# When the stores of a streaming attention kernel are let go: in pairs, each pair behind the K load eight groups later, instead of only the last nine, behind the last K load

## The chip, the cores and the metric

The kernel runs on one core of one Trainium2 chip. The metric is device time in microseconds (us). A program on one core is timed several times. The profiled execution has a "span" of its own, from its first to its last instruction; it is 1.8 us shorter than the device time in most kernels here, and 2.0 to 2.1 us in four of them (see e11). In the profile PE is TensorE (matrix products; PEld are its weight loads), DVE is VectorE, ACT is ScalarE, POOL is GpSimd and SP is SyncE, which only issues transfers here.

## The reference

```python
def reference(Q, K, V):                       # each (8, 12, 512, 64), float32
    Q_feat = np.maximum(0, Q)
    K_feat = np.maximum(0, K)
    KV = np.einsum('bhkd,bhkv->bhdv', K_feat, V)
    K_sum = np.sum(K_feat, axis=2)
    numerator = np.einsum('bhqd,bhdv->bhqv', Q_feat, KV)
    denominator = np.einsum('bhqd,bhd->bhq', Q_feat, K_sum)
    return (numerator / (denominator[:, :, :, None] + 1e-10)).astype(np.float32)
```

The work is light: 37.75 MB are read, 12.58 MB are written, and each byte is used once.

## The kernel before

The 96 heads are worked in 24 groups of four. A group has three loads (K, V, Q, each 512 KB of float32 in HBM, cast to bf16 on the way in) and one store (512 KB). The loads are issued by GpSimd, except for K and V of the first two groups; there are 14 buffers of each kind, so they run far ahead of the compute. The last step of a group is its "norm": DVE divides by the denominator and writes the output tile, which is then stored. The stores are issued by SP, in order.

```python
    HELD = 7
    # ...
    outp = pool("outp", HELD + 4)
    # ...
    for g in range(F32):                       # groups 0 and 1 come in as float32
        k_sb[g] = outp.tile([P, R, D], fp32, name="k_first", tag="o_sb")
        nc.sync.dma_start(out=k_sb[g]..., in_=Kr[g])
        # ... V likewise, issued by ACT
    # ...
    for g in range(2, NG - 2):
        load_kv(g)
        load_q(g)
    load_kv(NG - 2); load_kv(NG - 1); load_q(NG - 2); load_q(NG - 1)
    # ...
    def store(g, o_sb):
        if g == NG - 2 - HELD:                                     # g == 15
            nc.sync.dma_start(out=scratch, in_=k_sb[NG - 1][0:1, 0, :])
        parts = 2 if g >= NG - 3 else 1
        n = R // parts
        for j in range(parts):
            rs = slice(n * j, n * (j + 1))
            nc.sync.dma_start(out=Or[g].rearrange(...)[:, rs], in_=o_sb[:, rs])
    # ...
    for g in range(NG):
        mm_kv(g); evac_kv(g)
        # ... prep(g + 1): relu of K and copy of V, on DVE
        if g > 0:
            mm_out(g - 1)
            store(g - 1, norm(g - 1))
        transp(g); evac_qt(g)
    mm_out(NG - 1)
    store(NG - 1, norm(NG - 1))
```

The line with `scratch` is a gate. It copies 128 bytes of a K tile to a tile nobody reads. The copy has to wait until that tile is loaded, and since SP issues in order, all stores behind it wait too. Before, stores 0 to 14 go as soon as they are computed; stores 15 to 23 wait for K23, the last K load.

## Time and profile before

| | before |
|---|---|
| device time, median of the first runs | 130.9 us |
| busy share of the span: PE, DVE, ACT | 56%, 62%, 39% |
| share of the chain of waits that is DMA | 79% |
| K8 / K22 / K23 landed at | 42.7 / 109.7 / 112.9 us |
| first store issued at | 16.0 us |
| last norm ends at | 122.7 us |
| last store lands at | 128.4 us |

The first fence is from the profile page of the kernel before. It has the strips of 40 slices (3.2 us each) with the DMA engines' busy tenths and GB/s, the chain of waits by engine, and two DMA queues. q0 are the loads from GpSimd, q1 all that SP issues.

```profile
DMA  3999999999999999999999999999999999989991
GB/s 115 385 291 210 208 186 277 283 224 274 235 260 275 232 274 260 236 286 244 252 286 231 264 274 232 276 259 237 285 212 208 208 212 207 207 262 395 404 390 75
...
q0 software_dynamic: 9792, 17.83, 74.2%
q1 hardware_dynamic: 4208, 13.63, 27.9%
...
DMA 79%; DVE 5%; PE 3%; POOL 3%; issue 2%; ACT 2%; POOLq 0%; ACTq 0%
```

DMA is busy for eight tenths or more of every slice but the first and the last. The GB/s of the strip count a cast load at its bf16 size, so 210 for loads alone is 420 GB/s read from HBM; stores count once. Read so, loads alone and stores alone move nearly the same HBM bytes per us.

The second fence is from the table by stretches of time, kernel before. After the stretch come its length, the busy us and number of instructions of PE, PEld, DVE, ACT and POOL, and the granted clock. The last two columns, the ones used here, are the DMA share and GB/s. The share adds up the times of all packets of the sixteen engines, and these overlap a little, so it can pass 1.

```profile
18.00:20.00 2.00, 1.20 (x52) 0.71 (x44) 1.56 (x4) 1.56 (x5) 0.53 (x1) 1.00 1.10 155
43.30:93.90 50.60, 31.88 (x719) 23.62 (x720) 31.90 (x90) 20.67 (x50) 16.39 (x30) 0.53 1.10 259
98.40:112.90 14.50, 11.03 (x272) 8.18 (x270) 12.33 (x36) 7.83 (x19) 3.75 (x8) 0.61 1.12 210
113.00:114.00 1.00, 0.44 (x20) 0.23 (x16) 1.00 (x3) 0.39 (x2) 0.00 (x0) 1.00 0.73 135
114.00:115.00 1.00, 0.16 (x3) 0.17 (x4) 0.93 (x5) 0.00 (x0) 0.00 (x0) 1.00 0.69 195
...
118.00:122.00 4.00, 1.71 (x39) 1.18 (x36) 2.76 (x10) 1.02 (x1) 0.00 (x0) 0.50 1.01 402
122.00:124.00 2.00, 0.00 (x0) 0.00 (x0) 0.67 (x1) 0.00 (x0) 0.00 (x0) 0.50 1.02 389
...
126.00:127.00 1.00, 0.00 (x0) 0.00 (x0) 0.00 (x0) 0.00 (x0) 0.00 (x0) 0.50 0.64 244
127.00:128.00 1.00, 0.00 (x0) 0.00 (x0) 0.00 (x0) 0.00 (x0) 0.00 (x0) 0.50 0.07 27
```

Two dips stand out. At 18 to 20 us only loads run, at 155 instead of 210. The DMA share stays at 1.10 there, so the engines are not empty. At 113 to 115 us the share does fall, to 0.73 and 0.69: loads are running out, and the held stores have not begun. At the very end, 127 to 128, 27 GB/s is about the rate of a single engine, by an estimate from the 400 that sixteen make.

The third fence is SP's timeline of the kernel before (start, duration, what). It shows the gate.

```profile
0.74 0.86 SPq L87 DMA_DIRECT2D k_first<-in_K_dram  x2
15.95 71.68 SPq L184 DMA_DIRECT2D out_dram<-o_sb  x15
112.91 0.62 SPq L179 DMA_DIRECT2D scratch<-k_sb  x1
113.62 11.43 SPq L184 DMA_DIRECT2D out_dram<-o_sb  x12
```

### The profile page before, as it was taken

What the parts mean: (1) busy time and instruction counts of PE and PEld (TensorE: products, weight loads), DVE (VectorE), ACT (ScalarE), POOL (GpSimd) and SP (SyncE); (2) the same over time, 40 slices, a digit from 0 to 9 for tenths busy, and PEclk for the clock granted to TensorE, in tenths of its full rate; (3) what the DMA queues carried; (4) which work ended last, traced back from release to release, by engine and by line L of the source; (5) the groups of instructions that cost most, each with busy time, mean ns of one, the idle gap of its engine ahead of it and who ended that gap; (6) DMA issues with size and microseconds to landing.
All of it is one profiled execution on the core that took longest, in us unless ns stands there. A gap on an engine that the chain in (4) does not pass through costs nothing.

```text
span 129.3 us, 4118 instructions
## 1 busy us (share of the span) xinstructions
PE 73.0 (56%) x1728; PEld 54.3 (42%) x1728; DVE 80.5 (62%) x230; ACT 51.0 (39%) x121; POOL 39.2 (30%) x74
## 2 busy tenths in 40 slices
PE   0037982628565573585585665854856888556300
PEld 0036752416443452463364454533643656434200
DVE  1358883736757658458467576584586898897600
ACT  3034763333354335334533543353335366536000
POOL 6905343133433324315133333141333431000000
PEclk9999999755568559555555555555555555995555
DMA  3999999999999999999999999999999999989991
GB/s 115 385 291 210 208 186 277 283 224 274 235 260 275 232 274 260 236 286 244 252 286 231 264 274 232 276 259 237 285 212 208 208 212 207 207 262 395 404 390 75
DMA packets 14305, 32.76 MB, mean 253 GB/s; under 512 B 1616, under 2 KB 1616, under 8 KB 14288
## 3 DMA queue, kind: packets, MB, share of 16 engines
q0 software_dynamic: 9792, 17.83, 74.2%
q1 hardware_dynamic: 4208, 13.63, 27.9%
q10 hardware_dynamic: 288, 1.05, 2.1%
q8 instruction: 13, 0.21, 0.6%
q14 instruction: 4, 0.03, 0.1%
HBM read 37.75 MB, written 12.58 MB: 389 GB/s over the span
## 4 chain that ended last, share of the span: by engine, by line
DMA 79%; DVE 5%; PE 3%; POOL 3%; issue 2%; ACT 2%; POOLq 0%; ACTq 0%
DMA v_sb<-in_V_dram 41%; DMA q_sb<-in_Q_dram 27%; DMA k_sb<-in_K_dram 11%; DVE o_sb L168 2%; ACT qt L143 2%; PE ps_out L154 1%; POOL q_sb L82 1%; PE ps_qt L139 1%; DVE vo L116 1%; DVE rec L167 1%; PE ps_kv L124 1%; POOL k_sb L76 1%; POOL v_sb L78 1%; DVE den L165 0%; POOL ident masks.py:199 0%
## 5 line engine op out<-in xcount | busy, mean ns | idle before, releaser
L124 PE MATMUL ps_kv<-vo,kf 64*128 64x65 bf16 x768 | 23.3, 228 | 33.6 <-DVE vo L116 33.4
L133 ACT CAST kvd<-ps_kv 64x130 bf16<-64x130 f32 x96 | 25.4, 264 | 32.7 <-PE ps_kv L124 30.7
L143 ACT ACTIVATE qt<-ps_qt 128x1024 bf16<-128x1024 bf16 x24 | 24.6, 1024 | 34.4 <-PE ps_qt L139 34.4
L124 PEld LDWEIGHTS <-kf 64*128 64x128 bf16 x768 | 19.7, 119 | 39.2 <-DVE vo L116 31.5
L154 PE MATMUL ps_out<-kvd,qt 128*32 128x130 bf16 x768 | 27.9, 296 | 12.0 <-DVE o_sb L168 7.1
L168 DVE TENSOR_TENSOR o_sb<-ps_out,rec 128x512 f32<-128x512 f32 x48 | 33.2, 692 | 1.7
L114 DVE TENSOR_SCALAR kf<-k_sb,mask 128x1024 bf16<-128x1024 bf16 x44 | 19.4, 483 | 21.5 <-DMA k_sb<-in_K_dram 21.4
L154 PEld LDWEIGHTS <-qt 128*32 128x32 bf16 x768 | 17.1, 124 | 20.4 <-DVE o_sb L168 12.1
L82 POOL DMA_DIRECT2D q_sb<-in_Q_dram x24 | 15.2, 632 | 32.1 <-DMA k_sb<-in_K_dram 16.0
L139 PE MATMUL ps_qt<-ident,q_sb 128*128 128x128 bf16 x192 | 23.6, 299 | 2.2 <-DMA q_sb<-in_Q_dram 2.2
L139 PEld LDWEIGHTS <-q_sb 128*128 128x128 bf16 x192 | 17.5, 135 | 6.7 <-issue 3.8
L78 POOL DMA_DIRECT2D v_sb<-in_V_dram x22 | 11.7, 531 | 18.5 <-DMA q_sb<-in_Q_dram 11.2
L76 POOL DMA_DIRECT2D k_sb<-in_K_dram x22 | 11.9, 540 | 16.8 <-DMA v_sb<-in_V_dram 7.1
L116 DVE COPY vo<-v_sb 128x1024 bf16<-128x1024 bf16 x22 | 9.5, 430 | 9.4 <-DMA v_sb<-in_V_dram 9.4
L167 DVE RECIPROCAL rec<-den 128x8 f32<-128x8 f32 x48 | 9.8, 203 | 1.7
L165 DVE TENSOR_SCALAR den<-ps_out 128x8 f32<-128x8 f32 x48 | 7.6, 158 | 1.6 <-PE ps_out L154 1.6
L114 DVE TENSOR_SCALAR kf<-k_first,mask 128x1024 bf16<-128x1024 f32 x4 | 2.8, 750 | 5.3 <-DMA k_first<-in_K_dram 5.3
L133 ACT ACT_TABLE_LOAD x1 | 1.3, 1283 | 1.7 <-DVE kvd L107 1.7
L116 DVE CAST vo<-v_first 128x1024 bf16<-128x1024 f32 x2 | 1.4, 692 | 0.0
L105 DVE MEMSET mask<- 32x1 f32 x8 | 0.3, 59 | 0.9 <-PEq L216 0.8
L107 DVE MEMSET kvd<- 128x260 f32 x3 | 0.8, 275 | 0.0
masks.py:199 POOL TENSOR_SCALAR_AFFINE_SELECT ident<-ident 128x128 bf16<-128x128 bf16 x1 | 0.3, 287 | 0.1
(6 smaller groups left out, 0.8 us busy)
## 6 DMA issues: line engine op xcount, KB each, us to landing
out_dram<-o_sb SPq DMA_DIRECT2D x21, 512.0 KB, 6.7
q_sb<-in_Q_dram POOLq DMA_DIRECT2D x24, 256.0 KB, 12.4
k_sb<-in_K_dram POOLq DMA_DIRECT2D x22, 256.0 KB, 13.7
v_sb<-in_V_dram POOLq DMA_DIRECT2D x22, 256.0 KB, 13.4
out_dram<-o_sb SPq DMA_DIRECT2D x6, 256.0 KB, 4.2
v_first<-in_V_dram ACTq DMA_DIRECT2D x2, 512.0 KB, 6.6
k_first<-in_K_dram SPq DMA_DIRECT2D x2, 512.0 KB, 6.3
scratch<-k_sb SPq DMA_DIRECT2D x1, 0.1 KB, 3.3
```

What stands on the lines that cost most here:

```text
L76: nc.gpsimd.dma_start(out=k_sb[g].rearrange("p r d -> p (r d)"), in_=Kr[g])
L78: nc.gpsimd.dma_start(out=v_sb[g].rearrange("p r d -> p (r d)"), in_=Vr[g])
L82: nc.gpsimd.dma_start(out=q_sb[g].rearrange("p u f -> p (u f)"), in_=Qr[g])
L114: nc.vector.tensor_scalar(kf[g][:, :, s, :], k_sb[g], scalar1=0.0, scalar2=mask[:, s:s + 1], op0=Alu.max, op1=Alu.mult)
L116: nc.vector.tensor_copy(vo[g % NB][:, :, 0:D], v_sb[g])
L124: nc.tensor.matmul(ps_kv[g][:, t, 0:D1], kf[g][ts_, r, :, :].rearrange("p s d -> p (s d)"), vo[g % NB][ts_, r, :], start=(r == 0), stop=(r ...
L133: nc.scalar.copy(kvd[g % NB][64 * c:64 * c + 64, :, s, c, :], ps_kv[g][64 * s:64 * s + 64, :, 0:D1])
L139: nc.tensor.transpose(ps_qt[g][:, u, :], q_sb[g][:, u, :], ident)
L143: nc.scalar.activation(qt[g].rearrange("p u q -> p (u q)"), ps_qt[g].rearrange("p u q -> p (u q)"), Act.Relu)
L154: nc.tensor.matmul(po[hs, v // 2, (v % 2) * 2 * D1:(v % 2) * 2 * D1 + 2 * D1], qt[g][:, u, hs], kvd[g % NB][:, h // 2, h % 2, :, :], start ...
L167: nc.vector.reciprocal(rec, den)
L168: nc.vector.tensor_tensor(o_sb[:, 8 * j:8 * j + 8].rearrange("p (b r) d -> p b r d", b=2), pv[:, :, :, 0:D], rec.unsqueeze(3).to_broadcast ...
```

## The change

Its intent is to hold every store back a little, and to let none wait for the very end. Even-numbered stores 0 to 14 each get a gate on the K load eight groups later; the odd one behind it follows freely. So stores go in pairs from K8 on, and everything from store 14 on is free once K22 has landed. The output pool grows by one buffer, and the store of group 20 is split in two like those after it.

```diff
-    HELD = 7
+    DELAY = 8
...
-    outp = pool("outp", HELD + 4)
+    outp = pool("outp", DELAY + 4)
...
     def store(g, o_sb):
-        if g == NG - 2 - HELD:
-            nc.sync.dma_start(out=scratch, in_=k_sb[NG - 1][0:1, 0, :])
-        parts = 2 if g >= NG - 3 else 1
+        if g + DELAY < NG and g % 2 == 0:
+            nc.sync.dma_start(out=scratch, in_=k_sb[g + DELAY][0:1, 0, :])
+        parts = 2 if g >= NG - 4 else 1
```

## The prediction

> **What bounds the kernel now.** The DMA engines. The 40-slice strip shows DMA at 9 tenths from the second slice to the last but one; PE is busy 56%, DVE 62%, ACT 39%; the chain of waits is 79% DMA. A 512 KB transfer costs about the same in every phase, by the spacing of the K loads in the timeline: loads alone (K19 to K23) take 3.75 us a group of three, 1.25 us each; loads with one store a group (K8 to K18) 5.12 us, so a store costs 1.37 us; the nine held stores at the end run at 390 to 407 GB/s, 1.31 us each. HBM traffic is about 414 GB/s with and without stores. The Trainium skill's page "DMA: Bandwidth & Descriptors" (section "Queues, rings and completion order") says each engine round-robins between queues by packet; the trace agrees: with both busy, loads get about 195 GB/s of reads and stores 203.
>
> **What the change does.** It removes no byte. It adds 7 dummy transfers of 128 B (eight for one), each behind a K load. It splits the store of group 20: half stores run at 390 GB/s against 401, about 0.04 us. It moves work:
> - Before, stores 0 to 14 go as they are computed, from 16.0 us; 15 to 23 wait for K23, which lands at 112.9.
> - After, loads run alone up to K8: K2 at 12.1 + 6 x 3.75 = about 34.6 us, against 42.7 before. Then stores go in pairs, two for six loads, 10.2 us a pair; K22 lands at about 109 (109.7 before), and stores 14 to 23 follow freely.
>
> **How much is critical.** The order of transfers changes, not their sum, so little. To be won:
> 1. At the hand-over (113 to 115.5) the DMA rate falls to 194 to 304 GB/s: loads run dry before the held stores start, as K23's landing is seen late and a store's data comes about 1 us after its issue. Worth about 0.7 us. After, stores are released 3 us earlier, with V22 to Q23 in flight, so this dip should go.
> 2. A dip at 18 to 20 us (about 300 GB/s, 0.5 us lost), which may vanish or recur elsewhere.
>
> Against this: packets end at 126.5 on all but one engine, at 128.1 on a straggler. If that engine never starved in the dips, filling them gains nothing. I count half of the 0.7 us. At the end, Q23 shares with stores and lands at about 117.5 to 118 instead of 116.0; from the last transposes to the last norm takes 5 us (117.7 to 122.7), so compute ends at about 123 instead of 122.7, while the queue holds stores until about 126: still hidden. Buffers: norm g needs store g-12, released at K(g-4): no wait.
>
> **Prediction.** 130.9 - 0.4 = 130.5 us; 8 in 10: 129.2 to 131.7. Faster by over 2%: 0.06; within 2%: 0.90; slower: 0.04.
>
> **What would show each step.** K8 near 34.6, first store issued right after; K spacing 3.75 before, about 10.2 a pair after; K22 near 109. No dip under 350 GB/s between 109 and 118; no norm waits for a store; compute ends near 123; stores alone near 400 GB/s to about 126; total DMA packet time unchanged.
>
> **What would make it wrong.** A stretch of unmixed loads that DVE (3.4 us busy a group) or PE can't keep up with, so that loads wait for buffers; paired stores with more or less than half the share; a late Q23 that leaves the queue empty at the end (slower by 1 to 2 us); or a straggling engine, on which the end hangs, that gains or loses by the new order and that I can't name from the profile.

## The result

The changed kernel took 129.85 us (median of 4 runs, 129.79 to 130.14) where the kernel before took 130.8 (4 runs, 130.7 to 130.97). The ratio is 0.993, with a 95% interval of 0.9911 to 0.995. Ratios here are the mean time of one kernel's runs over that of the other's of the same rounds, so not quite the ratio of the quoted medians. It is within 2%, and clear of zero.

The page of the changed kernel, the lines that answer to the first fence:

```profile
DMA  3999999999999999999999999999999999999991
GB/s 109 380 299 212 208 211 209 211 210 209 210 209 260 303 223 241 305 236 232 305 246 211 310 264 211 291 283 209 235 307 242 228 311 246 230 386 411 404 362 67
...
q0 software_dynamic: 9792, 17.83, 74.6%
q1 hardware_dynamic: 4576, 13.63, 28.1%
...
DMA 79%; POOL 4%; PE 3%; DVE 3%; issue 3%; ACT 2%; POOLq 0%; ACTq 0%
```

Loads now run alone, at an even 210, in slices 4 to 12. Then pairs of stores show as bumps. Between the first slice and the last but one none is below 208. The same stretches as before in the table by time, changed kernel:

```profile
18.00:20.00 2.00, 1.22 (x51) 0.70 (x43) 1.53 (x4) 1.06 (x4) 0.53 (x1) 1.00 1.13 211
43.30:93.90 50.60, 32.12 (x704) 23.75 (x704) 31.60 (x89) 20.05 (x48) 16.26 (x30) 0.50 1.10 256
98.40:112.90 14.50, 8.44 (x208) 6.14 (x208) 10.06 (x30) 5.21 (x14) 1.80 (x4) 0.62 1.11 258
113.00:114.00 1.00, 0.66 (x7) 0.66 (x8) 0.93 (x4) 0.00 (x0) 0.00 (x0) 0.50 1.05 389
114.00:115.00 1.00, 1.00 (x30) 0.81 (x30) 0.83 (x2) 0.53 (x1) 0.00 (x0) 0.50 1.05 389
...
124.00:125.00 1.00, 0.00 (x0) 0.00 (x0) 0.00 (x0) 0.00 (x0) 0.00 (x0) 0.50 0.63 244
125.00:126.00 1.00, 0.00 (x0) 0.00 (x0) 0.00 (x0) 0.00 (x0) 0.00 (x0) 0.50 0.38 145
126.00:127.00 1.00, 0.00 (x0) 0.00 (x0) 0.00 (x0) 0.00 (x0) 0.00 (x0) 0.50 0.11 43
```

Both dips are gone (211 and 389). In exchange the end is no longer sharp: the rate falls in steps from 124 to 127 us, as one engine after another runs out. SP's timeline of the changed kernel:

```profile
35.51 0.61 SPq L179 DMA_DIRECT2D scratch<-k_sb  x1
36.17 1.85 SPq L184 DMA_DIRECT2D out_dram<-o_sb  x2
45.85 0.51 SPq L179 DMA_DIRECT2D scratch<-k_sb  x1
46.46 1.00 SPq L184 DMA_DIRECT2D out_dram<-o_sb  x2
...
107.73 0.50 SPq L179 DMA_DIRECT2D scratch<-k_sb  x1
108.32 13.86 SPq L184 DMA_DIRECT2D out_dram<-o_sb  x14
```

K8 landed at 35.5, K22 at 107.7, K23 at 110.4, Q23 at 115.9 us. The last norm ends at 121.2, and the last store lands at 126.95.

A transfer reports its completion sixteen times, once from each DMA engine. These records show the end engine by engine. For the last store of the program they are, in us after the first of the sixteen:

```
before:  first at 126.8, last at 128.4, mean 127.1
  0.0 0.0 0.0 0.0 0.1 0.1 0.1 0.1 0.1 0.1 0.2 0.2 0.3 0.6 0.6 1.6
changed: first at 124.2, last at 126.9, mean 125.4
  0.0 0.0 0.1 0.3 0.4 0.4 0.8 0.9 1.0 1.4 1.6 2.2 2.5 2.5 2.7 2.7
```

On average the engines finish 1.65 us earlier, the last one 1.44 us. That is one profile of each; the profile of before was one of its slower executions (131.08 us). By median device time the gain is 0.95 us.

The span ends only 1.25 us earlier (129.30 and 128.06): from the last landing to its end the changed kernel takes 1.11 us and the kernel before 0.91. In all runs with 40 transfers (see below) this is 1.09 to 1.11; one of SP's last steps, a drain, comes 0.5 us after the wait in front of it instead of 0.1. Why, no run shows. So all gains of runs with 40 transfers against before are some 0.2 us smaller than what is won up to the last landing.

### The profile page after: what moved, and what is told of

Its sections match the earlier page's. It is cut to its first block, busy times and chain, and to the rows that moved or that the text cites. A ratio compares the mean times of both kernels' runs of the same rounds, so it can differ in the third digit from the quotient of the medians.

```text
span 128.1 us, 4127 instructions
## 1 busy us (share of the span) xinstructions
PE 73.7 (58%) x1728; PEld 54.9 (43%) x1728; DVE 80.3 (63%) x230; ACT 51.0 (40%) x121; POOL 39.4 (31%) x74
## 4 chain that ended last, share of the span: by engine, by line
DMA 79%; POOL 4%; PE 3%; DVE 3%; issue 3%; ACT 2%; POOLq 0%; ACTq 0%
DMA q_sb<-in_Q_dram 41%; DMA v_sb<-in_V_dram 30%; DMA k_sb<-in_K_dram 8%; DVE o_sb L168 2%; ACT qt L143 2%; PE ps_qt L139 1%; POOL q_sb L82 1%; POOL v_sb L78 1%; PE ps_out L154 1%; PE ps_kv L124 1%; POOL k_sb L76 1%; DVE vo L116 1%; DVE rec L167 1%; DVE den L165 0%; POOL ident masks.py:199 0%
## 5 line engine op out<-in xcount | busy, mean ns | idle before, releaser
L124 PE MATMUL ps_kv<-vo,kf 64*128 64x65 bf16 x768 | 24.1, 233 | 32.8 <-DVE vo L116 32.3
L124 PEld LDWEIGHTS <-kf 64*128 64x128 bf16 x768 | 20.5, 122 | 38.3 <-DVE vo L116 30.3
```

The costliest lines, as they stand in the source:

```text
L124: nc.tensor.matmul(ps_kv[g][:, t, 0:D1], kf[g][ts_, r, :, :].rearrange("p s d -> p (s d)"), vo[g % NB][ts_, r, :], start=(r == 0), stop=(r ...
```

## The experiments

The theory going in was "tail": the gain is the dip at the hand-over from loads to stores (113 to 115 us), filled because stores are let go while the last loads are still under way. Its rivals were "start" (the gain is the dip of 18 to 20 us, which went when the first store moved from 16 to 36 us) and "pairing" or "even mixing" (it matters that stores are spread in pairs over all loads). A fourth, "semaphore", came up on the way.

All kernels below gave correct results. Each call's kernels ran on one chip with the kernel before. Differences are between the means of the runs; "this" has 5 or 6 of them, "before" 11.

| run | what is left of the change | us, mean | against before | ratio, 95% interval |
|---|---|---|---|---|
| e1_tail22 | tail only | 130.34 | -0.38 | 0.9972 (0.9955 to 0.9989) |
| e2_start8 | start only, 33 transfers | 130.69 | -0.03 | 0.9998 (0.9975 to 1.0021) |
| e3_free | no gate at all | 134.44 | +3.72 | 1.0285 (1.0262 to 1.0307) |
| e4_start8_tail22 | both ends, 33 transfers | 130.43 | -0.29 | 0.9979 (0.996 to 0.9998) |
| e5_after_again | all | 129.91 | -0.81 | 0.9941 (0.9925 to 0.9957) |
| e6_pairs_tail23 | start and pairs, no tail | 129.95 | -0.76 | 0.9945 (0.9928 to 0.9962) |
| e7_pairs_split3 | all but the split of store 20 | 129.69 | -1.03 | 0.9924 (0.9906 to 0.9943) |
| e8_two_gates | both ends, 34 transfers | 130.41 | -0.31 | 0.998 (0.9961 to 0.9998) |
| e9_ends_same_count | both ends, 40 transfers | 129.99 | -0.68 | 0.9949 (0.9929 to 0.997) |
| e10_start_same_count | start only, 40 transfers | 130.18 | -0.49 | 0.9964 (0.9943 to 0.9985) |
| e11_before_plus_one | before, 33 transfers | 131.54 | +0.88 | 1.0071 (1.0048 to 1.0094) |
| e12_start4_same_count | store 0 behind K4 only, 40 transfers | 130.65 | -0.02 | 0.9999 (0.9981 to 1.0018) |

"Transfers" are those issued by SP and ACT; why their number matters is told with e8, e9 and e11.

### First call: the two ends apart

**e1_tail22**, the tail alone, from the kernel before:

```diff
         if g == NG - 2 - HELD:
-            nc.sync.dma_start(out=scratch, in_=k_sb[NG - 1][0:1, 0, :])
+            nc.sync.dma_start(out=scratch, in_=k_sb[NG - 2][0:1, 0, :])
```

> Before with one change: the last nine stores wait for K22 instead of K23, so only the hand-over at the end is filled. Tail theory (the gain of the change, about 0.9 us, is the filled dip at the end): 0.5 to 0.9 us faster than before, no dip between 109 and 118, the dip at 18 to 20 us still there. Start theory (the gain is the dip of 18 to 20 us that went): within 0.2 us of before. Even-mixing theory (the gain comes from stores spread evenly over all loads): within 0.2 us of before.

It is 0.38 us faster, short of the expected 0.5 to 0.9. The dip of 18 to 20 us is still in its profile, the one at the hand-over is gone. So filling the hand-over is worth something, but by these means it is less than half of the change.

**e2_start8**, the start alone, from the kernel before:

```diff
+        if g == 0:
+            nc.sync.dma_start(out=scratch, in_=k_sb[8][0:1, 0, :])
         if g == NG - 2 - HELD:
```

> Before with one change: store 0, and so all stores behind it, waits for K8; the end is as before. Start theory: the dip at 18 to 20 us is gone and the kernel is 0.4 to 0.9 us faster. Tail theory: within 0.2 us of before, the dip of 113 to 115.5 is still there even if that of 18 to 20 us is gone. Even-mixing theory: within 0.2 us of before or slower.

There is no difference in time: by the expectations, a clear vote against "start". It was not one. The dip of 18 to 20 us is gone from its profile, and its mean span is 0.31 us shorter than before's of the same rounds, though the device time is not. Something at the end ate the gain; see e8.

**e3_free**, from the kernel before:

```diff
-        if g == NG - 2 - HELD:
-            nc.sync.dma_start(out=scratch, in_=k_sb[NG - 1][0:1, 0, :])
```

> Before without any gate: each store goes when it is computed. Tail theory: no hand-over dip, as there are always stores, but the last loads share with stores and stores alone are few at the end, so the last group's compute is exposed: slower than before by 1 to 4 us, and DMA falls to low tenths in the last slices. Start theory: the dip of 18 to 20 us is there; not faster than before. Even-mixing theory: as fast as the changed kernel or faster.

It is 3.72 us slower: without any gate the cost is real, and it is the expected one. Q23 lands at 122.7 us instead of 116.0, since stores share with loads to the end. The table by time and PE's timeline of this run show what follows:

```profile
121.00:123.00 2.00, 1.49 (x28) 1.30 (x30) 1.66 (x4) 0.36 (x1) 0.00 (x0) 0.50 0.65 214
123.00:125.00 2.00, 1.82 (x55) 1.45 (x50) 0.54 (x3) 1.69 (x5) 0.00 (x0) 0.50 0.57 211
125.00:127.00 2.00, 0.83 (x12) 0.56 (x13) 1.49 (x4) 1.02 (x1) 0.00 (x0) 0.50 0.34 128
...
121.51 1.03 PE L139 MATMUL ps_qt<-ident,q_sb 128*128 128x128 bf16 x8 [1.93 <-DMA q_sb<-in_Q_dram]
```

From 121 us on the DMA engines are a third to two thirds busy, waiting for the compute of the last two groups. So in this kernel holding stores back pays: it keeps a reserve of stores for the time when nothing else is left to move.

**e4_start8_tail22** has both edits, of e1 and of e2.

> Both parts without the pairing: store 0 waits for K8, the last nine for K22. If the two dips add up, the time is that of the changed kernel (0.7 to 1.2 us faster than before). If only the tail matters, it is that of the run with the tail alone. If the even pairing matters by itself, it stays 0.4 us or more behind the changed kernel.

No gain over e1 (-0.29 against -0.38), although its profile shows neither dip and its last store lands at 126.9 us, as in the changed kernel. At this point "pairing" looked best.

### Second call: parts taken out of the changed kernel

**e5_after_again** is the changed kernel, unaltered, for a comparison on one chip.

> The changed kernel once more, unaltered, so that it can be set against its parts on one chip. If its 0.7% of the first job holds, 0.8 to 1.0 us faster than before and the profiled span near 128.1 us. If part of that was the chip or the luck of few runs, 0.4 to 0.6 us, which is what the run with only the tail filled gave.

The gain holds: 0.81 us.

**e6_pairs_tail23** takes the tail away from the changed kernel:

```diff
         if g + DELAY < NG and g % 2 == 0:
-            nc.sync.dma_start(out=scratch, in_=k_sb[g + DELAY][0:1, 0, :])
+            kg = NG - 1 if g + DELAY == NG - 2 else g + DELAY
+            nc.sync.dma_start(out=scratch, in_=k_sb[kg][0:1, 0, :])
```

> The changed kernel with one edit: stores 14 to 23 wait for K23 as in the kernel before, instead of K22; the gates of stores 0 to 12 stay. Tail theory: the hand-over dip comes back, some engines run dry between 112 and 116 us, and 0.4 to 0.7 us of the gain are lost. Even-mixing theory: the gain stays, within 0.2 us of the changed kernel.

It loses only 0.05 us. As an account of the whole gain, "tail" is refuted. A dip at the hand-over does come back in its profile, but a shallower one than before's: adding up, from 109 to 118 us, what is missing to 410 GB/s of HBM traffic (loads at their float32 size, each packet's bytes spread evenly over its record), it costs 0.29 us of full rate, against 0.80 in before. These are single profiles, and dips vary: with before's gate the sum is 0.49 in e11 and 0.63 in e2. With the ten stores from 14 on behind K23 it is 0.29 in e6, 0.32 in e10 and 0.39 in e12.

**e7_pairs_split3** is the changed kernel with `parts = 2 if g >= NG - 3`, as before.

> The changed kernel with the store of group 20 whole, as before. By half stores at 390 GB/s against 401 this is 0.04 us of work; both theories expect it within 0.2 us of the changed kernel. If it is 0.3 us slower or more, the split at the end carries part of the gain.

As expected the split carries none of the gain. This version had the lowest time, 129.69 us against 129.91 of the changed kernel on the same chip; single runs overlap (129.49 to 129.96, and 129.73 to 130.03), as do the intervals of the ratios, so I take 0.2 us as a hint. It has 39 transfers, so its last store has the last place but one in the row told of next; its trace takes 0.98 us from the last landing to the end of the span, 0.11 less than that of e5.

**e8_two_gates** takes out the pairs in between:

```diff
-        if g + DELAY < NG and g % 2 == 0:
-            nc.sync.dma_start(out=scratch, in_=k_sb[g + DELAY][0:1, 0, :])
+        if g == 0 or g == NG - 2 - DELAY:
+            nc.sync.dma_start(out=scratch, in_=k_sb[8 if g == 0 else NG - 2][0:1, 0, :])
```

> The changed kernel with the gates of stores 2 to 12 taken out; those of stores 0 (K8) and 14 (K22) stay, and the buffers and splits too. If only the two ends matter (no dip at 18 to 20, none at the hand-over), it equals the changed kernel within 0.2 us. If the pairs in between matter by themselves, it is 0.3 us slower or more and lands near 130.4 us.

It lands at 130.41, just where "pairing" said. But its profile has no dip either. The program ends with SP waiting, in a fixed order, for the eight semaphores that its transfers take in turn. The transfers of SP and ACT number 32 in the kernel before (27 stores, 4 first loads, 1 gate) and 40 in the changed one (28, 4, 8): both are multiples of eight, so the last store has the semaphore that is waited for last. In e2 and e4 it is 33, and in e8 34; there the last store has the first or second place, and the rest of the row is walked after it has landed. So the experiments that dropped gates had moved the end of the program as well. The last waits of e8, from the waits view:

```profile
SPq L227 <- DMA out_dram<-o_sb: 4.5, 2, 3.9
```

Two waits, the second until the last store has landed, and six places of the row still to come. What that costs can be taken off from e8's own numbers. It is 0.50 us slower than e5 (the changed kernel on the same chip). Of this 0.24 us lie outside the span, and 0.17 between the last landing and the end of the span (1.26 against 1.09, in the two traces). That leaves 0.1 us, within noise, for the six gates taken out.

### Third call: the count held fixed

**e11_before_plus_one** tests this by itself, on the kernel before:

```diff
+        if g == 1:
+            nc.sync.dma_start(out=scratch, in_=k_sb[2][0:1, 0, :])
         if g == NG - 2 - HELD:
```

> Before with one idle 128-byte transfer more, behind store 1, that waits for no load. Semaphore theory: 33 transfers, the last store takes the first place in the row of the last waits, so 7 waits of 0.06 us follow its landing: 0.4 to 0.7 us slower than before, 1.3 us from the last landing to the end of the span instead of 0.9. Pairing theory: within 0.1 us of before.

One transfer of 128 bytes that waits for no load makes the kernel 0.88 us slower, more than the 0.4 to 0.7 expected. These are SP's last waits, from the trace of each (start in us, semaphore):

```
before, last store lands at 128.39        e11_before_plus_one, last store lands at 127.98
126.48  S[115]                            128.00  S[108]   <- the last store's
127.14  S[116]                            128.06  S[109]
127.78  S[117]                            128.12  S[111]
128.41  S[118]   <- the last store's      128.18  S[112]
128.48  drain                             128.24  S[115]
                                          128.30  S[116]
                                          128.36  S[117]
                                          128.42  S[118]
                                          128.49  drain
```

The waits view says the same: in the kernel before SP's final line waits five times, for 2.8 us in all and 0.6 at most; in e11 once, for 3.0 us, until the last store has landed, with seven waits still to come. First the kernel before, then e11:

```profile
SPq L227 <- DMA out_dram<-o_sb: 2.8, 5, 0.6
```

```profile
SPq L229 <- DMA out_dram<-o_sb: 3.0, 1, 3.0
```

From the last landing to the end of the span it is 1.34 us here (1.34 in e4, 1.33 in e2, 1.26 in e8) against 0.91 in before: 0.43 us, seven waits of 0.06. Besides, the device time of e2, e4, e8 and e11 exceeds the mean span by 2.03 to 2.06 us, that of all others by 1.77 to 1.82. This further 0.25 us lies outside the span and I have no explanation for it. The two together are 0.68 of the 0.88 us; the rest is open. The extra transfer may also disturb the start: in the one trace of e11 the dip there costs 0.89 us of full rate (17 to 25 us), in that of before 0.61.

**e9_ends_same_count** is e8 again with the gates in between kept as dummies, which read a K tile that has long landed. In the changed kernel:

```diff
         if g + DELAY < NG and g % 2 == 0:
-            nc.sync.dma_start(out=scratch, in_=k_sb[g + DELAY][0:1, 0, :])
+            kg = {0: 8, 14: 22}.get(g, g)
+            nc.sync.dma_start(out=scratch, in_=k_sb[kg][0:1, 0, :])
```

> The run with two gates once more (store 0 behind K8, store 14 behind K22), but with the six dummies in between kept: they read a K tile that landed long before and wait for no load. So the number of transfers on SP and ACT is 40 as in the changed kernel, and the last store has the semaphore that the end of the program waits for last. Semaphore theory (the run with two gates was slow because its 34 transfers gave the last store an early place in the fixed row of the last waits): 0.6 to 1.0 us faster than before, as the changed kernel, 0.06 us from the last landing to the last wait's end. Pairing theory: stays near 0.2 us faster than before.

It is 0.68 us faster than before, where e8, with the same two gates on loads that bind, was 0.31 faster. (The expectation of 0.06 us named the wait itself; from the last landing to the end of the span it is 1.09 us, as in the changed kernel, 1.11.) Between this and the changed kernel (-0.81 on another chip) the intervals overlap for the most part.

One thing in e9 is not as intended. The dummies wait for no load, but all write the same tile, so each waits until the one before it has landed:

```profile
SPq L180 <- DMA scratch<-k_sb: 18.6, 5, 5.1
```

That is five waits of up to 5.1 us, and SP's timeline shows the stores going in pairs, 5 to 7 us apart, up to 65 us. So e9 drops the spread of pairs over all K loads (one pair in 10.3 us), but not every pairing. The dummies of e10 and e12 are of the same kind. e8 has no dummies at all, issues 14 stores in a row without a gate, and is within 0.1 us of the changed kernel once its end is taken off. The two together leave no clear sign of "pairing", though an effect of 0.1 to 0.3 us could hide in the noise: what looked like its effect in e4 and e8 was, for the most part, the place of the last store in the row of waits, by the number of transfers modulo eight.

**e10_start_same_count** has `{0: 8, 14: 23}` in that place: the start alone.

> Start alone, at the same count of 40: store 0 behind K8, stores 14 to 23 behind K23, the dummies in between wait for nothing. Start theory: 0.5 to 0.9 us faster than before. Pairing theory: within 0.2 us of before, as the first run of the start alone was.

0.49 us faster, just under the 0.5 to 0.9 that "start" expected. This is what e2 should have shown.

**e12_start4_same_count** has `{0: 4, 14: 23}`: store 0 waits for K4 only.

> As the start alone, but store 0 waits for K4 (lands near 20 us) instead of K8, so only the first store moves, by some 4 us. If the gain at the start is the dip of 18 to 20 us, made by the first store's early issue, the dip goes and the time is that of the start alone. If it comes from the long stretch of loads alone up to K8, the time stays within 0.3 us of before, or the dip comes back near 22 to 24 us.

No gain at all, and the dip is back, some 5 us later. Stretches of this run:

```profile
18.00:20.00 2.00, 1.25 (x47) 0.70 (x40) 1.47 (x4) 1.05 (x4) 0.53 (x1) 1.00 1.12 209
23.00:25.00 2.00, 1.57 (x36) 1.13 (x37) 1.31 (x4) 0.83 (x4) 0.65 (x2) 0.50 1.09 159
```

and of e10:

```profile
18.00:20.00 2.00, 1.16 (x40) 1.03 (x43) 1.60 (x6) 0.12 (x2) 0.86 (x2) 0.56 1.13 212
23.00:25.00 2.00, 1.62 (x49) 1.00 (x43) 1.88 (x6) 1.59 (x5) 0.84 (x2) 0.50 1.11 209
```

The two kernels differ in one number, 4 or 8, and in 0.47 us. As e12 has all the dummies, the split and the ten held stores too, it also shows that these together gain nothing without the gate on K8. When the first store comes early, the loads under way slow down for about 2 us, shortly before the store's own data begins to move (16.0 issued, 20 us moving, in before). When it comes behind K8 there is no such dip, though its data again begins to move some 4 us after its issue (36.2 and 40 us in the changed kernel). Why an early first store does this no run here shows. Nor is the dip told apart from its rival in the expectation of e12, a gain from the long stretch of loads alone up to K8: in that text a dip that comes back counts for the stretch. In all runs the stretch and the missing dip go together, and no gate between K4 and K8 was tried. What is shown is that the gate on K8 gains 0.47 us over one on K4, and that the dip goes with it.

## Why the prediction was right, and where its sizes were off

- **DMA bounds the kernel, and the order of transfers costs nothing in itself.** Right. In the mixed stretch of 43 to 94 us the rate is 259 before and 256 after (with loads at their float32 size, 410 GB/s of HBM traffic in both), and e9 and, with its end taken off, e8 match the changed kernel.
- **The hand-over dip goes (0.7 us, half of it counted).** The mechanism is right, and its size is right where nothing else is changed: e1 gained 0.38 us against 0.35 counted. On top of the start gate it is worth less: 0.19 us between e9 and e10, 0.05 between e5 and e6, neither clear of noise. There the dip itself is shallower: 0.29 and 0.32 us of full rate are missing in e6 and e10, 0.80 in before.
- **The dip at 18 to 20 us "which may vanish or recur elsewhere", counted as nothing.** This is the term that was mis-sized. It vanished, and the gate that takes it away is worth 0.47 to 0.49 us (e10 against e12 and before), the larger part of the gain. The prediction had named its size (0.5 us lost) but credited none of it. It did recur in e12, where the first store moved by 4.9 us only.
- **The straggler.** Right that it matters. Before, fifteen engines report the last store within 0.6 us and one 1.6 us after the first; after, they are spread over 2.7 us. The time hangs on the last one; that filling a dip helps only the engines starved or slowed in it is my reading, as the traces do not name a packet's engine. Summed over 10 to 122 us as for e6, the changed kernel regained 1.55 us of full rate over before, and 0.81 to 0.95 us of time. e1 and e10 each regained 1.1 us of rate and 0.4 to 0.5 us of time, but e12 regained 0.4 and no time (-0.02; the 0.2 us lost after the last landing is in this). So between nothing and some 60% comes through in these single profiles; half, as the prediction counted for the one dip, is no rule.
- **K8 near 34.6, K22 near 109, 10.2 us a pair.** Measured 35.5, 107.7 and 10.3 (72.2 us for seven pairs). K8 was 0.9 us late: the loads from K2 on came 3.9 us apart, not 3.75. K22 was 1.3 us early against the predicted 109, but this 109 does not follow from the prediction's own terms: 34.6 and seven pairs of 10.2 make 106.0. Another estimate fits better: 14 stores are ahead of K22 instead of 15, one store less is 1.37 us at the prediction's price, the saved dip is 0.5, so 109.7 - 1.9 = 107.8. It may fit by chance, as K22's sixteen completions spread over 5.2 us in this trace.
- **Q23 at 117.5 to 118, compute ends near 123.** Off: 115.9 and 121.2. K22 was early already, and the loads behind it needed 8.2 us where the prediction had 8.5 to 9. It was hidden either way, with stores queued until 124 us.
- **Total packet time unchanged.** Nearly: load packets took 94.69 us per engine before and 94.14 after. All runs with the start dip have 94.45 to 94.98, all without it 94.14 to 94.19. That is the dip: packets that took longer, not missing ones.
- **Total.** 0.4 us predicted; 0.95 measured in the first job and 0.81 in the second. The time was inside the range because the range was wide: 129.2 to 131.7 holds both dips, and also no change at all. So the hit says little. The gain was about twice the one named, and that the hand-over came out at just the 0.35 us counted is in part luck, as "half" was a guess.

## What to carry to other kernels

In a kernel bound by DMA, look for the stretches in which the rate drops and price each separately; the sum of bytes does not change by reordering, but a dip can be filled. Measure what it brings: here between nothing and some 60% of what was filled reached the end time. Hold some stores back for the end (none held cost 3.7 us), release them before the last loads have drained (0.38 us in e1), and do not let the very first store out into a young load stream without looking at what it does (0.47 us between e12 and e10). When an experiment removes or adds transfers, keep their number the same modulo the semaphores in turn, or compare what happens after the last landing: otherwise an effect of 0.4 to 0.9 us at the end can pass for a cause. And see what a dummy that keeps the number waits for itself.

## What the Trainium skill lacked or had wrong

- "DMA: Bandwidth & Descriptors", section "Queues, rings and completion order", says each engine round-robins between queues by packet. The runs fit this: with both queues busy, loads and stores get 193 and 203 GB/s of HBM traffic in before (50 to 52 us). The page does not say that the first store issued early into a stream of loads slows these: 155 instead of 210 on the strip's scale, for 2 us, with packets of up to 499 ns instead of 173 (before; in e12 159 and up to 615 ns).
- No page says how far the sixteen engines drift apart over a kernel: the completions of one transfer spread over 0.7 us at the first cast loads of before, 2.8 at its last loads, and in the changed kernel 5.2 at K22 and 2.7 at the last store. "Runtime: NRT & Kernel Launch", section "Instruction fetch mechanics", says instruction memory is refilled in 16 KiB blocks by DMA. The trace agrees: 13 transfers of 16,384 bytes in before, 0.88 to 0.97 us each, on a queue of their own (q8). That they land on single engines and so make part of the drift is my guess from the spreads; no run tested it. The page calls the cost mostly hidden.
- No page says that the end of a program can wait for the transfers' semaphores in a fixed order, so that the last transfer's place in it costs up to seven waits of 0.06 us after its landing (e11: 1.34 us from landing to end instead of 0.91), nor what the other 0.25 us outside the profiled span are, nor what takes 0.2 us more at the end of the span with 40 transfers.
